# Upper conditioning groups as VectorE sums, bias with the small vectors, two context banks opened by halves

## Chip, cores and metric

The kernel runs on one core of a Trainium2 chip. Its time is the device time of one execution in microseconds; lower is better. The time before is the median of three runs.

## The reference

One layer (DEPTH = 1) of a trunk over 2048 latent positions of width 1024, with 256 context positions in front. The part that the change touches is the conditioning at the start:

```
ada   = silu(c)     @ w_ada + b_ada      # six vectors of 1024: sh1, sc1, g1, sh2, sc2, g2
ada_c = silu(c_ctx) @ w_ada + b_ada      # csh1, csc1, ... for the context
hc = rmsnorm(ctx, norm_mix) * (1 + csc1) + csh1
hf_c, hb_c = states of the scans over  hc @ w_in[:, :3*512]
h  = rmsnorm(x, norm_mix) * (1 + sc1) + sh1
x  = x + g1 * (token_mixers(h @ w_in, start states hf_c, hb_c) @ w_out)
...                                      # then the gated MLP with a 3x3 convolution, and a final RMSNorm
```

So nothing can be multiplied by w_in before shift (sh1) and scale (sc1) are there, and the context comes first: its two states start the latents' scans.

## The kernel before

**Conditioning.** The columns of w_ada for shift and scale are four groups of 512: groups 0 and 1 are the shift's lower and upper half, 2 and 3 the scale's. Each is loaded as two tiles of 1 MB (`load_ada`, L252). The two vectors silu(c) and silu(c_ctx) stand in `cs2`, index w = 1 for the context. Groups 0, 2 and 3 are products on TensorE with two rows out (`ada_products`, L263); `ada_columns` (L269) adds the bias row on VectorE, transposes the sum into columns and `put_ada` (L282) writes them into `s1` (shift) or `a1` (scale, times the norm's gain). Group 1 is summed on VectorE (`ada_sums`, L276): for each of eight k one scalar_tensor_tensor for w = 0 and one for w = 1 into `acc`, whose first partition is loaded with the bias; eight products with a matrix of ones then sum over partitions. A pair of columns k = 0 to 3 of 128 features needs groups 0 and 2, and k = 4 to 7 needs groups 1 and 3.

**Context.** Two tiles of context rows are squared on ScalarE (`x_square`), scaled on VectorE (`x_scale`, L227) and transposed into four PSUM banks (`pct`). `ctx_mod` (L293) applies shift and scale to column k (`x_mod`: `xfl`, L232, on VectorE), rounds it to fp32r on ScalarE (`ch`, L120) and takes the rest as `cl` (L121), on GpSimd for k below 4 and on VectorE above. All products are three fp32r products of such high and low parts. `split_w` does the same for 128 columns of w_in: `whi` on ScalarE, `wlo` on VectorE or GpSimd.

**Banks.** `run_banks` (L481) then goes through a list of output banks: twelve of the context, each 24 products of 256 columns (`pj<-ch,...`), among them from the seventh on the first of the latent (`pj<-xh,...`, 512 columns). Between products it calls `slot()`, which runs tasks of two queues (`hg_q`, `bg_q`) when the sum of modelled product times has come to their due time. One task, `x_start` with `x_first` (L371), squares, scales (`xg`, L227), transposes and modulates the first 1024 latent rows.

**Order.** The start stands in a block `manual_schedule`, where the written order is kept for the instructions of that block; what comes after it is placed by a scheduler, engine by engine, and may also be placed between the block's instructions. Loads of weights and rows go through SyncE's queue, the small vectors through ScalarE's. A `raw` buffer (three of them) holds context rows at first and weights of w_in after.

Of the kernel before, what the change touches and what calls it, by code (L numbers as in the profile page):

```python
# [9 lines left out]
F32 = mybir.dt.float32  # L10
# [62 lines left out]
def tile_trunk(ctx, tc, x, c, cx, c_ctx, w_ada, b_ada, norm_mix, norm_ffn, w_in, hg_norm, sgu_g, sgu_b,  # L73
# [104 lines left out]
    with es1:  # L178
# [70 lines left out]
        acc = ph.tile([P, 2, 512], F32, tag="S", name="acc")  # L249
        G.memset(acc, 0.0)  # L250

        def load_ada(g, qs=(0, 1)):  # L252

            for q in (qs,) if isinstance(qs, int) else qs:
                t = wa[g // 2][:, 4 * (g % 2) + 2 * q:4 * (g % 2) + 2 * q + 2, :]
                wts[g, q] = t.rearrange("p a (b e) -> p (a b) e", e=512)
                ld(wts[g, q], wv[:, 4 * q:4 * q + 4, g * 512:(g + 1) * 512])

        def load_bias(g, tag):
            rows[g] = pm.tile([2, 512], F32, tag=tag, name="rows", bufs=2)  # L260
            ld(rows[g], b_ada[0:1, g * 512:(g + 1) * 512].broadcast_to([2, 512]))
# [6 lines left out]

        def ada_columns(g):  # L269
            V.tensor_add(rows[g], rows[g], pa.pop(g)[:2, :])  # L270
            pv = bank("pj")
            for j in range(4):
                T.transpose(pv[:, 2 * j:2 * j + 2], rows[g][:, j * P:(j + 1) * P], ident[:2, :2])
            put_ada(g, [pv[:, w:8:2] for w in range(2)])

        def ada_sums(k0, k1):  # L276
            for k in range(k0, k1):
                for w in range(2):
                    V.scalar_tensor_tensor(out=acc[:, w, :], in0=wts[1, k // 4][:, k % 4, :], scalar=cs2[:, k, w:w + 1],
                                           in1=acc[:, w, :], op0=ALU.mult, op1=ALU.add)  # L280

        def put_ada(g, cols):  # L282
            sl = slice(4 * (g % 2), 4 * (g % 2) + 4)
            for w in range(2):
                if g < 2:
                    V.tensor_copy(s1[:, w, sl], cols[w])
                else:
                    V.scalar_tensor_tensor(out=a1[:, w, sl], in0=cols[w], scalar=1.0, in1=nmix[:, sl],
                                           op0=ALU.add, op1=ALU.mult)
# [4 lines left out]
        def ctx_mod(k, eng):  # L294
            x_mod(pct[k // 2][:, (k % 2) * 256:(k % 2) * 256 + 256], 1, k, chl[:, k, :], cll[:, k, :], CTX, eng)
# [4 lines left out]
        with tc.manual_schedule():  # L300
# [3 lines left out]
            vr = pm.tile([50, P], F32, tag="gu", name="vr", bufs=2)  # L304
            for a, n, r0 in ((norm_mix[0], 8, 0), (norm_ffn[0], 8, 8), (hg_norm[0], 4, 16), (sgu_g[0], 4, 20),
                             (sgu_b[0], 4, 24), (conv_b[0], 22, 28)):
# [5 lines left out]
            load_bias(0, "ot")  # L312
            for w in range(2):
                ld(acc[0:1, w, :], b_ada[0:1, 512:1024])
            load_bias(3, "vv")
            load_ada(3)
            load_raw((0, CTX))
# [5 lines left out]
            pv = bank("sc")  # L323
            T.transpose(pv[:, :50], vr, ident[:50, :50])
            V.tensor_copy(vec, pv[:, :50])
            ada_products(2, 1)
            ada_columns(2)
            x_scale(xc, ss, keep=lambda i: i)
            ada_sums(0, 4)
            ada_products(0, 0)  # L330
# [4 lines left out]
            load_raw((HW, CTX))  # L335
            ada_products(0, 1)
            ada_columns(0)
            ada_sums(4, 5)
            for k in range(4):
                ctx_mod(k, G)  # L340
                if k == 1:
                    ada_sums(5, 6)
            ada_products(3, 0)
# [3 lines left out]
            ada_sums(6, 8)  # L347
# [1382 lines left out]
```

## Time and profile before

| | |
|---|---|
| median of three runs | 2520.57 us (2520.07 to 2527.65) |
| the profiled execution, its own time | 2514.66 us |
| its span | 2512.8 us, mean granted TensorE clock 0.991 |
| PE busy | 2442.2 us (97%) |
| DVE busy | 1800.0 us (72%) |
| ACT, POOL busy | 957.3 us (38%), 1055.6 us (42%) |
| DMA | 400.13 MB, mean 159 GB/s |
| first context product on PE | 43.03 us from the span's start |

How to read it: the span runs from the first instruction to the last of one profiled execution. PE is TensorE (matmul), DVE VectorE, ACT ScalarE, POOL GpSimd, SP SyncE. A timeline row gives start, duration, engine, line, operation, output and inputs by the program's names, shapes and count; the bracket gives the idle time before it and what ended that. A row of windows gives for a stretch each engine's busy time with its number of instructions, then the granted TensorE clock (PEclk, 1.00 is full), the DMA engines' share and the rate. A product of fp32 shows as two MATMUL instructions, one of fp32r as one.

### The profile page before, as it was taken

The page shows a single profiled execution, that of the slowest core. Times are in us where ns is not written, and L with a number is a line of the kernel's source. Part 1 is how long each engine was busy: PE and PEld are TensorE (multiplying, and loading weights), DVE is VectorE, ACT ScalarE, POOL GpSimd, SP SyncE. Part 2 cuts the span into 40 slices and gives each one's busy share as a digit, 9 for nine tenths or more (in the row PEclk, how much of TensorE's full clock was granted, in tenths as well). Part 3 has the DMA queues.
Part 4 walks back from the last instruction along what each step waited for, and adds up shares of the span by engine and source line. Part 5 has one row for each costly group of instructions (what it writes and reads, how often), then busy time and mean ns, then how long its engine had stood idle before and what let it go on. Part 6 is the DMA issues. An engine that isn't in the chain of part 4 may idle for free.

```text
span 2512.8 us, 32811 instructions
## 1 busy us (share of the span) xinstructions
PE 2442.2 (97%) x11859; PEld 2021.4 (80%) x11859; DVE 1800.0 (72%) x2375; ACT 957.3 (38%) x1598; POOL 1055.6 (42%) x871
## 2 busy tenths in 40 slices
PE   7999999999999999999999999999999999999998
PEld 4787888788888788788778888878878887888886
DVE  5867875745665666465799778759999993676775
ACT  2553334433334343245443333324333343332352
POOL 1344232232333333100588787877878870000002
PEclk8999999999999999999999999999999999999999
DMA  8365445573353422668832222472222249844744
GB/s 293 96 194 181 131 130 193 177 248 126 101 180 104 148 88 97 237 210 256 301 106 87 90 79 89 148 261 85 82 92 87 94 134 343 275 148 134 232 159 149
DMA packets 307839, 400.13 MB, mean 159 GB/s; under 512 B 33106, under 2 KB 216138, under 8 KB 304606
## 3 DMA queue, kind: packets, MB, share of 16 engines
q1 hardware_dynamic: 304420, 397.30, 47.6%
q8 instruction: 94, 1.54, 0.2%
q10 hardware_dynamic: 3257, 0.75, 0.1%
q14 instruction: 68, 0.55, 0.1%
HBM read 288.85 MB, written 109.13 MB: 158 GB/s over the span
## 4 chain that ended last, share of the span: by engine, by line
PE 38%; DVE 7%; DMA 3%; POOL 2%; issue 2%; ACT 0%; SPq 0%; POOLq 0%; ACTq 0%; DVEq 0%
PE up L65 24%; PE dn L65 14%; DVE dn L1318 4%; DMA mr<-m 1%; DVE edges L1323 1%; DMA raw<-in_w_up_dram 1%; POOL Al L121 1%; DVE gp L1394 0%; DMA yl<-yd 0%; DMA sT<-wd 0%; DVE mhl L121 0%; DVE odd L1598 0%; POOL raw L1145 0%; POOL fl L1141 0%; ACT dn L1615 0%
## 5 line engine op out<-in xcount | busy, mean ns | idle before, releaser
L1318 DVE SCALAR_TENSOR_TENSOR dn<-gp,taps,dn 128x1024 f32<-128x1024 f32 x352 | 448.3, 1280 | 20.6 <-ACT dn L1315 17.4
L121 POOL TENSOR_TENSOR Al<-raw,Ah 128x512 fp32r<-128x512 f32 x264 | 344.9, 1315 | 97.5 <-ACT Ah L120 91.3
L65 PE MATMUL pj<-xh,whi 128*128 128x512 f32 x896 | 364.7, 407 | 0.5 <-ACT xh L120 0.5
L65 PE MATMUL pj<-xl,whi 128*128 128x512 f32 x896 | 351.2, 392 | 1.9 <-DVE xl L121 1.1
L65 PE MATMUL pj<-xh,wlo 128*128 128x512 f32 x896 | 350.9, 392 | 1.0 <-DVE wlo L121 1.0
L65 PE MATMUL dn<-th,mhl 128*128 128x512 f32 x1120 | 347.4, 391 | 2.2 <-ACT mhl L120 0.9
L65 PE MATMUL up<-xah,Ah 128*128 128x512 f32 x704 | 277.0, 394 | 1.6 <-ACT Ah L120 1.2
L65 PE MATMUL up<-xah,Al 128*128 128x512 f32 x704 | 276.3, 392 | 1.8 <-POOL Al L121 1.8
L65 PE MATMUL up<-yl,Ah 128*128 128x512 f32 x704 | 274.5, 390 | 1.9 <-DMA yl<-yd 1.9
L120 ACT CAST Ah<-raw 128x512 fp32r<-128x512 f32 x264 | 160.5, 618 | 296.1 <-PE up L65 236.3
L65 PEld LDWEIGHTS dn<-th,mhl 128*128 128x128 f32 x1120 | 210.2, 188 | 50.7 <-ACT mhl L120 1.3
L121 POOL TENSOR_TENSOR wlo<-raw,whi 128x1024 fp32r<-128x1024 f32 x56 | 141.2, 2522 | 226.8 <-ACT whi L120 210.3
L113 POOL TENSOR_SCALAR rs<-ss 128x2 f32<-128x2 f32 (+1 forms) x16 | 7.7, 481 | 526.6 <-ACT jk L1590 361.4
L65 PE MATMUL dn<-tl,mhl 128*128 128x512 f32 x560 | 219.8, 392 | 0.0
L65 PE MATMUL up<-yh,Ah 128*128 128x512 f32 x528 | 208.1, 394 | 0.0
L65 PE MATMUL up<-yh,Al 128*128 128x512 f32 x528 | 206.9, 392 | 0.0
L65 PE MATMUL up<-xal,Ah 128*128 128x512 f32 x528 | 205.5, 389 | 0.0
L65 PEld LDWEIGHTS pj<-xh,wlo 128*128 128x128 f32 x896 | 168.5, 188 | 37.6 <-DVE wlo L121 1.7
L65 PEld LDWEIGHTS pj<-xh,whi 128*128 128x128 f32 x896 | 169.4, 189 | 34.3 <-issue 3.5
L65 PEld LDWEIGHTS pj<-xl,whi 128*128 128x128 f32 x896 | 169.3, 189 | 33.2 <-DVE xl L121 2.1
L65 PE MATMUL dn<-wo,o 128*128 128x512 f32 x768 | 182.6, 394 | 0.9 <-DVE nt L672 0.9
L65 PEld LDWEIGHTS dn<-wo,o 128*128 128x128 f32 x768 | 142.0, 188 | 30.1 <-issue 1.1
(321 smaller groups left out, 4675.0 us busy)
## 6 DMA issues: line engine op xcount, KB each, us to landing
raw<-in_w_up_dram SPq DMA_DIRECT2D x88, 512.0 KB
mr<-m SPq DMA_DIRECT2D x85, 512.0 KB
raw<-in_w_in_dram SPq DMA_DIRECT2D x68, 512.0 KB
sT<-wd SPq DMA_DIRECT2D x88, 256.0 KB
raw<-in_w_ada_dram SPq DMA_DIRECT2D x32, 512.0 KB
m<-cv SPq DMA_DIRECT2D x22, 544.0 KB
raw<-in_w_down_dram SPq DMA_DIRECT2D x22, 512.0 KB
wd<-raw SPq DMA_DIRECT2D x22, 512.0 KB
```

The source lines that it names most:

```text
L65: return self.engine.matmul(out, lhsT, rhs, **kw)
L113: keep(G.tensor_scalar(out=r[:, :n], in0=ss, scalar1=scale, scalar2=bias, op0=ALU.mult, op1=ALU.add))
L120: keep(S.copy(hi, raw))
L121: (eng or G).tensor_sub(lo, raw, hi.bitcast(F32))
L1318: V.scalar_tensor_tensor(out=cr, in0=gt[:, t // 3:t // 3 + RH, t % 3:t % 3 + GW], scalar=taps[:, t * NF + f:t * NF + f + 1], in1=cr, op0=A ...
L1323: V.scalar_tensor_tensor(out=e[:, 0, :], in0=gt[:, 1, t % 3:t % 3 + GW], scalar=taps[:, t * NF + f:t * NF + f + 1], in1=e[:, 0, :], op0=AL ...
```

## The change

Groups 1 and 3 are both summed on VectorE now, separately for the context's vector (w = 1) and the latent's (w = 0), each with ones products of its own (`ada_ones`); the two accumulators stand in `acc[1]` and `acc[3]`. Groups 0 and 2 stay on TensorE, and ScalarE copies their rows. The bias of all four groups is loaded with the small vectors (`vr`, now 66 rows), transposed with them and kept in columns (`bc`), where `put_ada` adds it. The latent's sums of group 3 are written behind the block as five tasks of `hg_q` (`last_sums`).

The context's lower columns (k below 4) are modulated and rounded on ScalarE; all `cl` are on VectorE. The first two context banks (columns 0 and 512) are opened with k = 0 to 3 inside the block (`ctx_products`), and `run_banks` finishes them with k = 4 to 7. Their weights are split on VectorE, and loaded ahead of groups 1 and 3.

```diff
-        acc = ph.tile([P, 2, 512], F32, tag="S", name="acc")
-        G.memset(acc, 0.0)
+        acc = {1: ph.tile([P, 2, 512], F32, tag="S", name="acc1"),
+               3: view(ph.tile([P, NCH + 1, P], F32, tag="bst", name="acc3"), 0, [[512, 2], [1, 512]])}
+        for g in (1, 3):
+            G.memset(acc[g], 0.0)
...
+                for k in range(0, 4, 2 if (g, q) == (3, 1) else 4):
+                    e = 4 if (g, q) != (3, 1) else k + 2
+                    ld(wts[g, q][:, k:e, :], wv[:, 4 * q + k:4 * q + e, g * 512:(g + 1) * 512])
...
+        def ada_rows(g, tag):
+            rows[g] = pm.tile([2, 512], F32, tag=tag, name="rows", bufs=2)
+            S.copy(rows[g], pa.pop(g)[:2, :])
+
         def ada_columns(g):
-            V.tensor_add(rows[g], rows[g], pa.pop(g)[:2, :])
-            pv = bank("pj")
+            o = 128 + 16 * g
             for j in range(4):
-                T.transpose(pv[:, 2 * j:2 * j + 2], rows[g][:, j * P:(j + 1) * P], ident[:2, :2])
-            put_ada(g, [pv[:, w:8:2] for w in range(2)])
+                T.transpose(small[:, o + 2 * j:o + 2 * j + 2], rows[g][:, j * P:(j + 1) * P], ident[:2, :2])
+            put_ada(g, small[:, o:o + 8].rearrange("p (j w) -> p w j", w=2), 0, 2)
-        def ada_sums(k0, k1):
+        def ada_sums(g, w, k0, k1):
             for k in range(k0, k1):
-                for w in range(2):
-                    V.scalar_tensor_tensor(out=acc[:, w, :], in0=wts[1, k // 4][:, k % 4, :], scalar=cs2[:, k, w:w + 1],
-                                           in1=acc[:, w, :], op0=ALU.mult, op1=ALU.add)
+                V.scalar_tensor_tensor(out=acc[g][:, w, :], in0=wts[g, k // 4][:, k % 4, :], scalar=cs2[:, k, w:w + 1],
+                                       in1=acc[g][:, w, :], op0=ALU.mult, op1=ALU.add)
+        def ada_ones(g, w, to, o):
+            for j in range(4):
+                T.matmul(to[:, o + 2 * j:o + 2 * j + 2], acc[g][:, w, j * P:(j + 1) * P], ones[:, :2], start=True, stop=True)
+            put_ada(g, to[:, o:o + 8].rearrange("p (j u) -> p u j", u=2)[:, :1, :], w, w + 1)
+        def put_ada(g, cols, w0, w1):
             sl = slice(4 * (g % 2), 4 * (g % 2) + 4)
+            dst = (s1, a1)[g // 2][:, w0:w1, sl]
+            V.tensor_add(dst, cols, view(bc, 4 * g, [[0, w1 - w0], [1, 4]]))
+            if g > 1:
+                V.tensor_mul(dst, dst, view(vec, sl.start, [[0, w1 - w0], [1, 4]]))
...
-        def ctx_mod(k, eng):
-            x_mod(pct[k // 2][:, (k % 2) * 256:(k % 2) * 256 + 256], 1, k, chl[:, k, :], cll[:, k, :], CTX, eng)
+        def ctx_mod(k):
+            pt = pct[k // 2][:, (k % 2) * 256:(k % 2) * 256 + 256]
+            sc, sh = a1[:, 1, k:k + 1], s1[:, 1, k:k + 1]
+            fl = pm.tile([P, 512], F32, tag="sig", name="xfl", bufs=2)
+            if k < 4:
+                S.activation(fl[:, :CTX], pt, AF.Identity, bias=sh, scale=sc)
+                S.copy(chl[:, k, :], fl[:, :CTX])
+            else:
+                V.tensor_scalar(out=fl[:, :CTX], in0=pt, scalar1=sc, scalar2=sh, op0=ALU.mult, op1=ALU.add)
+                S.activation(chl[:, k, :], pt, AF.Identity, bias=sh, scale=sc)
+            V.tensor_sub(cll[:, k, :], fl[:, :CTX], chl[:, k, :].bitcast(F32))
...
-            load_bias(2, "ot")
-            for q in range(2):
-                load_ada(0, q)
-                load_ada(1, q)
...
+            load_ada(0)
+            load_raw((0, CTX))
+            load_ada(1)
+            load_raw((HW, CTX))
             load_ada(3)
-            load_raw((0, CTX))
...
             ada_products(2, 1)
+            ada_rows(2, "ot")
+            x_scale(xc, ss, keep=lambda i: i)
+            ada_products(0, 0)
             ada_columns(2)
...
+            nxt[0, CTX] = split_w((0, CTX), V)
             (16 transposes of the context)
             ada_products(0, 1)
+            ada_rows(0, "ot")
+            ada_sums(1, 1, 0, 8)
             ada_columns(0)
+            ada_ones(1, 1, small, 256)
+            for c in (0, HW):
+                opened[c, CTX] = bank("pj")
             for k in range(4):
+                ctx_mod(k)
+                ada_sums(1, 0, 2 * k, 2 * k + 2)
+                ctx_products(0, (k,))
+            nxt[HW, CTX] = split_w((HW, CTX), V)
+            ctx_products(HW, range(4))
+            ada_ones(1, 0, small, 272)
             load_raw((2 * HW, CTX))
...
+            ada_sums(3, 1, 0, 8)
+            ada_ones(3, 1, small, 288)
             for k in range(4, NK):
+                ctx_mod(k)
+        last_sums = [lambda k=k: ada_sums(3, 0, k, k + 2) for k in range(0, 8, 2)]
+        last_sums.append(lambda: ada_ones(3, 0, bank("mi"), 0))
...
+                pj = opened.pop(keys[i], None)
+                k0 = 0 if pj is None else 4
+                pj = pj or bank("pj")
...
+        for i in range(5):
+            hg_q.later(sums_now, 1.0 + 2.0 * i)
```

More of the change, by code (lines that the diff above doesn't have):

```diff
@@ L297, in tile_trunk, with ctx_products @@
+        opened = {}
+        def ctx_products(c, ks):
+            hi, lo, _ = nxt[c, CTX]
+            pj = opened[c, CTX]
+            for k in ks:
+                mm3(pj[:, :CTX], hi[:, k, :], lo[:, k, :], chl[:, k, :], cll[:, k, :], k == 0, False)
         xg = [ph.tile([P, D], F32, tag=t, name="xg", bufs=2) for t in ("vt", "vt", "sgt", "sgt")]
@@ L495, in run_banks @@
                 hiT, loT = (chl, cll) if n == CTX else (xh, xl)
-                pj = bank("pj")
+                pj = opened.pop(keys[i], None)
+                k0 = 0 if pj is None else 4
+                pj = pj or bank("pj")
                 sl = slice(n0, n0 + n)
-                for k in range(NK):
+                for k in range(k0, NK):
                     if k and n == 512:
```

56 lines of the change are left out of this document (14 added, 42 removed).

## The prediction

> **What bounds the kernel now.** I read the page first, for the limit of the whole, then the windows, for the stage that the change touches, then the timelines of PE, DVE, ACT and POOL there.
>
> ```profile
> span 2512.8 us, 32811 instructions
> PE 2442.2 (97%) x11859; PEld 2021.4 (80%) x11859; DVE 1800.0 (72%) x2375; ACT 957.3 (38%) x1598; POOL 1055.6 (42%) x871
> ```
> PE is the limit of the whole, with some 70 us idle. What delays PE early and is not made up stays in the end time.
>
> ```profile
> core 0: us, PE busy (x) PEld busy (x) DVE busy (x) ACT busy (x) POOL busy (x), PEclk, DMA share, GB/s
> 5.00:20.00 15.00, 12.39 (x27) 2.41 (x28) 2.44 (x6) 2.30 (x4) 0.92 (x2) 1.00 1.04 402
> 20.00:43.00 23.00, 17.94 (x67) 7.98 (x65) 17.44 (x24) 2.57 (x5) 6.92 (x5) 0.91 1.06 371
> 43.00:60.00 17.00, 16.34 (x84) 15.10 (x85) 9.52 (x21) 10.42 (x21) 0.19 (x1) 0.62 0.42 137
> 60.00:80.00 20.00, 16.65 (x118) 14.35 (x117) 18.62 (x28) 14.05 (x25) 11.19 (x6) 1.00 0.42 125
> 80.00:100.00 20.00, 17.43 (x104) 13.66 (x102) 17.80 (x30) 7.26 (x15) 6.42 (x6) 1.00 0.24 65
> ```
> To 43 us DMA is full; DVE has room before 20 (2.44 of 15) and is near its limit from 20 to 43. From 43 to 60 PE multiplies the context banks, at 0.62 of its clock. From 60 to 100 DVE is nearly full (18.62 and 17.80 of 20): the latent chain.
>
> ```profile
> start us, us, engine line op out<-in xcount [idle before <-releaser]
> 12.90 3.60 PE L65 MATMUL pj<-wa,cs 128*2 128x512 f32 x8
> 17.26 0.41 PE L69 MATMUL pj<-ident,rows 2*128 2x2 f32 x4 [0.77 <-DVE rows L270]
> 21.12 1.53 PE L69 MATMUL mi<-ident,raw 128*128 128x128 f32 x12
> 39.04 3.54 PE L65 MATMUL pj<-ones,acc 128*128 128x2 f32 x16 [3.56 <-POOL wlo L121]
> 43.84 0.41 PE L65 MATMUL pj<-ch,whi 128*128 128x256 f32 x1
> 44.05 0.41 PE L65 MATMUL pj<-cl,whi 128*128 128x256 f32 x1
> 55.56 0.41 PE L65 MATMUL pj<-ch,wlo 128*128 128x256 f32 x1
> 55.77 0.37 PE L65 MATMUL pj<-ch,whi 128*128 128x256 f32 x1
> 56.09 0.28 PE L65 MATMUL pj<-ch,wlo 128*128 128x256 f32 x1
> 56.21 0.28 PE L65 MATMUL pj<-ch,whi 128*128 128x256 f32 x1
> 74.29 0.48 PE L65 MATMUL pj<-xh,whi 128*128 128x512 f32 x1
> ```
> Starts of neighbours give the price of one context product: 0.21 us at 44, 0.12 at 56. The second bank's last (the 48th) starts at 55.56, the first latent product at 74.29.
>
> ```profile
> 22.09 5.39 DVE L279 SCALAR_TENSOR_TENSOR acc<-wa,cs,acc 128x512 f32<-128x512 f32 x8 [2.83 <-DMA acc<-in_b_ada_dram]
> 34.98 4.62 DVE L279 SCALAR_TENSOR_TENSOR acc<-wa,cs,acc 128x512 f32<-128x512 f32 x3
> 39.52 0.67 DVE L270 TENSOR_TENSOR rows<-rows,pj 2x512 f32<-2x512 f32 x1
> 43.13 0.23 DVE L288 SCALAR_TENSOR_TENSOR a<-pj,vec 128x4 f32<-128x4 f32 x2 [2.94 <-PE pj L69]
> 43.61 0.55 DVE L232 TENSOR_SCALAR xfl<-mi,a,s 128x256 f32<-128x256 f32 x1
> 44.62 0.43 DVE L121 TENSOR_TENSOR cl<-xfl,ch 128x256 fp32r<-128x256 f32 x1 [0.47 <-ACT ch L120]
> 44.97 0.54 DVE L232 TENSOR_SCALAR xfl<-mi,a,s 128x256 f32<-128x256 f32 x1
> 49.63 1.23 DVE L121 TENSOR_TENSOR wlo<-raw,whi 128x1024 fp32r<-128x1024 f32 x1 [0.52 <-ACT whi L120]
> 61.15 2.74 DVE L227 TENSOR_SCALAR xg<-xg,rs 128x1024 f32<-128x1024 f32 x4 [0.91 <-POOL rs L115]
> 241.79 1.53 DVE L872 SCALAR_TENSOR_TENSOR acc<-raw,cs,acc 128x512 f32<-128x512 f32 x2
> ```
> This is the chain to 43 us: sums that wait for a bias row until 22.09, then run slowly beside POOL (three in 4.62 us), then ones products and small copies, then the upper context columns (xfl) from 43.61, 1.36 us each.
>
> **The change part by part.** Of the changed kernel I use only the order in which its instructions stand on each engine. From about 100 us on the two orders are the same, so the change is worth what it moves before that: nothing behind is tied to a fixed time, and whom PE waits for there is as late as PE.
>
> *Removed:* group 3's two sets of PE products (2 x 3.6 us by the row at 12.90), three row additions of 0.67 us on DVE, the bias transfers with the 2.83 us stall, and POOL's subtractions, which slowed the sums. *Added on DVE:* 16 more sums, four cl subtractions and one wlo subtraction that POOL had. That is 16 x 0.66 + 4 x 0.34 + 1.2 = 13.2 us, less 4 x 0.45 for lower xfl that go to ACT and 2.0 for row additions: 9.4 us net, on the engine that the upper columns queue on. What stands against this is DVE's idle time before 43.
>
> Sums that alternate between two accumulators start 0.66 us apart (5.39 - 0.74, over 7); two on one accumulator take 1.53 for the pair, 0.79 apart.
>
> *Walk to the lower columns.* PE's second set ends at 16.5. Group 0's first half now follows at once (3.4, the row's 3.60 less the tail of its last product): 19.9, then four transposes: 20.3. Its weights have landed: 4 MB at 402 GB/s is 10.4 us from about 5. DVE, which waited, makes a1 to 20.8 and the first wlo (1.2) to 22.0. The context's eight upper-shift sums share one accumulator: 7 x 0.79 + 0.74 = 6.3, to 28.3. Ones products: 16 instructions took 3.54 us, at half clock; eight are 1.8, or 0.9 at full clock, which PE still has here: 29.2, s1 29.4. ACT makes the lower columns' ch beside this.
>
> *Walk to the upper columns.* DVE's queue now has four groups of one cl and three sums. The third sum is one of the latent's scale: all eight of these, written to run behind, stand in the built order ahead of the upper columns. 4 x (0.34 + 3 x 0.66) = 9.3: 38.7; wlo 1.2: 39.9; two sums: 41.3. Next is s1 from the second ones products, which PE has behind the half bank opened on column 512: 12 products after that wlo. At half clock 12 x 0.21 = 2.5 and 1.8: 44.3, s1 44.5, and DVE idles 3 us with ten sums queued behind. Those ten: five alternate, five follow on one accumulator, 7.3: 51.8. Ones products 1.8, two small operations: 54.0. So the first upper xfl starts at 54.0 against 43.61. Each column again costs 1.36, since in the built order ACT's ch still waits for xfl, and PE's six products for it (6 x 0.21 = 1.28) fit beside it: the last cl ends at 59.4, the 48th product near 60.4 against 55.56: 4.9 later. The 24 products done early save this much and no more.
>
> ```profile
> 35.48:38.90 3.42, 0.00 (x1) 0.00 (x0) 3.42 (x3) 0.00 (x0) 2.91 (x2) 1.00 1.02 411
> 49.14:52.55 3.41, 2.95 (x12) 2.63 (x12) 1.23 (x1) 2.96 (x6) 0.00 (x0) 0.50 0.08 25
> 55.96:59.37 3.41, 3.41 (x31) 3.41 (x30) 2.49 (x5) 3.38 (x6) 0.00 (x0) 1.00 0.61 192
> 441.67:445.08 3.41, 0.88 (x5) 0.88 (x6) 2.68 (x4) 2.05 (x5) 0.00 (x0) 1.00 0.62 197
> 445.08:448.49 3.41, 3.41 (x16) 3.22 (x15) 3.17 (x6) 1.00 (x2) 2.78 (x1) 0.50 0.43 161
> ```
> The clock: half after a stretch in which PE was busy 0.00 of 3.42 us, but also after one with 0.88 of 3.41. Between 29 and 40 the changed PE has three products of 0.21 every 2.3 us, about as little as that 0.88; so I take half clock there, and full again at some 59 to 60.
>
> The Trainium skill ("TensorE: Matmul & The Clock Gate", Part 1: The HAM clock gate) lets the clock fall only after an idle window of about 3.4 us. By that rule it would hold until 42 here and the second ones products would end some 2 us earlier; the row at 441.67 speaks against it.
>
> *The latent chain.*
>
> ```profile
> 58.47 1.06 ACT L221 ACTIVATE xjk<-xg 128x1024 bf16<-128x1024 f32 x1
> 59.53 0.35 ACT L554 COPY vv<-pj 128x256 f32<-128x256 f32 x1
> 59.78 1.05 ACT L120 CAST whi<-raw 128x1024 fp32r<-128x1024 f32 x1
> 60.06 1.06 POOL L115 TENSOR_TENSOR rs<-rs,mhalf 128x4 f32<-128x4 f32 x1
> ```
> Before, the last square (58.47) stands ahead of the third bank's vv, and the scaling of the latent rows (xg) starts at 61.15. In the changed order the last two squares stand behind that vv. The third bank starts after its weights are split (1.05 on ACT, which waits for the first bank's buffer): 60.4 + 1.4 + 24 x 0.12 = 64.7; vv, square, split, square (0.4 + 1.2 + 1.0 + 1.2) 68.5; POOL's two operations (1.06 and a shorter one) 1.4: scaling at 69.9, 9 us later. The first latent product, which waited for both before, then comes 5 later if PE's context banks set it and 9 later if the scaling does. The second latent chunk hangs on the same DVE queue, which is full, so lateness of scaling reaches it undiminished.
>
> *At nothing:* ACT's seventh small load, 0.3 us at 3 us (PE waits for weights until 7); POOL's second memset; w_ada's last MB in two pieces; the context's first weights ahead of group 1. The second weight load now stands on SP ahead of group 3 and waits for PE's transposes (21.12): group 3 lands near 31, and DVE needs its last part near 45. Without that cover DVE would wait as long as it lacks.
>
> Sum: +4.9 at two banks, 5 to 9 at the first latent product, 9 where DVE sets the pace; I take **+9.5**, near the scaling's lateness, since DVE is the full engine from 60 to 100, with ends of +5 and +14 (POOL's and DVE's collisions, which made three sums cost 4.62 for 2.0, can hit the squeezed chain again). The profiled execution took 2514.66 us (span 2512.8); the median of the runs is 2520.57. The difference adds to either; on the median: **2530**.
>
> **The rivals.** *A, the clock holds* (the skill's rule, above): second ones products and half bank at full clock save 1.1 + 0.9; +7.5, 2528. For: PE is never idle for a whole window between 29 and 40. Against: the row at 441.67. Chance 0.15.
>
> *B, PE's slack absorbs it, and it is not slower.* PE is idle 3.35 + 2.57 = 5.9 us from 60 to 100; if PE's work and not DVE sets the latent banks, the 4.9 at two banks is swallowed: -1, 2519.6. It decides by the scaling: at 64.5 or earlier (61.15 + 3.35). For: 24 context products are done by 43. Against: DVE 18.62 of 20, and my 69.9. Chance 0.13.
>
> *C, the squeezed chain collides.* POOL's and DVE's latent splits meet as DVE's sums met POOL's split at 34.98, 2.6 us each time; two or three times more than before: +14.7 to +17.3, 2535 to 2538. For: the splits crowd behind a later scaling. Against: before has such meetings too, and its sums lose theirs here. Chance 0.12.
>
> **How the numbers follow.** Forecast 0.60. A difference of 0.3% (7.6 us) is about what a measurement of this kernel can tell from no change. Slower: 0.45 of the forecast's 0.60 (its part above +7.6), half of A (0.07), C: 0.64. Within: the other 0.15, A's 0.08, most of B: 0.33. Faster: 0.03, if B also gains what POOL no longer slows. Range 2521 to 2537: from just above B's end well into C; what it leaves out is most of B and part of C.
>
> **What would show it.** Right: first upper xfl near 54, preceded by a chain of sums without an ACT or DMA wait; half clock between 32 and 59; scaling near 70; then a constant lag. Wrong: upper xfl before 50; scaling before 64.5; full clock through 29 to 42; a DMA as releaser of a sum of group 3.

## The result, and the profile after

The changed kernel takes 2535.56 us (median of four runs, 2534.25 to 2539.13) against 2520.32 us of the kernel before on the same chip: the ratio is 1.0057, with a 95% interval of 1.0041 to 1.0073, which is 10.3 to 18.4 us. It is slower, as forecast; the forecast was +9.5. The profiled execution took 2539.13 us, the highest of its four, and that of before 2514.66, below all four of its own; the two ends are therefore not compared, but marks in the first 130 us.

The page of the changed kernel, its span and its engines:

```profile
span 2537.3 us, 32818 instructions
PE 2443.8 (96%) x11855; PEld 2021.8 (80%) x11855; DVE 1809.6 (71%) x2392; ACT 960.2 (38%) x1604; POOL 1048.4 (41%) x867
```

PE is busy about as long as before (2442.2 us there): group 3's products are gone, but more of its work runs at half clock, as the next rows show. DVE has 9.6 us more, POOL 7.2 less: the sums and subtractions that moved.

Four of the windows that were shown of before, now of the changed kernel (length, then busy time of each engine, then the granted clock, the DMA share and the rate):

```profile
core 0: us, PE busy (x) PEld busy (x) DVE busy (x) ACT busy (x) POOL busy (x), PEclk, DMA share, GB/s
20.00:43.00 23.00, 13.50 (x62) 8.89 (x61) 19.65 (x32) 6.26 (x11) 0.00 (x0) 0.73 1.02 371
43.00:60.00 17.00, 7.78 (x35) 7.39 (x35) 11.41 (x22) 1.69 (x3) 0.00 (x0) 0.50 0.43 145
60.00:80.00 20.00, 17.01 (x119) 16.04 (x119) 13.88 (x28) 13.12 (x26) 1.86 (x3) 0.88 0.34 98
80.00:100.00 20.00, 16.50 (x105) 13.27 (x104) 16.00 (x20) 12.27 (x25) 10.56 (x7) 1.00 0.21 61
```

From 43 to 60, where PE was busy for 16.34 us before, it is busy for 7.78, at half clock: it waits for the upper context columns.

DVE's timeline up to those columns, and three marks behind them (start, duration, engine, line, operation, count; in brackets the idle time before and what ended it):

```profile
21.46 1.22 DVE L121 TENSOR_TENSOR wlo<-raw,whi 128x1024 fp32r<-128x1024 f32 x1 [0.93 <-ACT whi L120]
22.85 6.26 DVE L283 SCALAR_TENSOR_TENSOR acc<-wa,cs,acc 128x512 f32<-128x512 f32 x8 [0.17 <-DMA wa<-in_w_ada_dram]
30.39 0.16 DVE L294 TENSOR_TENSOR s<-sc,bc 128x4 f32<-128x4 f32 x1 [1.21 <-PE sc L65]
30.80 2.07 DVE L283 SCALAR_TENSOR_TENSOR acc<-wa,cs,acc 128x512 f32<-128x512 f32 x3
...
39.76 1.22 DVE L121 TENSOR_TENSOR wlo<-raw,whi 128x1024 fp32r<-128x1024 f32 x1
40.90 1.53 DVE L283 SCALAR_TENSOR_TENSOR acc<-wa,cs,acc 128x512 f32<-128x512 f32 x2
45.07 0.16 DVE L294 TENSOR_TENSOR s<-sc,bc 128x4 f32<-128x4 f32 x1 [2.64 <-PE sc L65]
45.15 7.33 DVE L283 SCALAR_TENSOR_TENSOR acc<-wa,cs,acc 128x512 f32<-128x512 f32 x10
54.50 0.16 DVE L294 TENSOR_TENSOR a<-sc,bc 128x4 f32<-128x4 f32 x1 [2.02 <-PE sc L65]
54.90 0.54 DVE L310 TENSOR_SCALAR xfl<-mi,a,s 128x256 f32<-128x256 f32 x1
56.41 0.54 DVE L310 TENSOR_SCALAR xfl<-mi,a,s 128x256 f32<-128x256 f32 x1
...
73.44 2.74 DVE L227 TENSOR_SCALAR xg<-xg,rs 128x1024 f32<-128x1024 f32 x4 [1.19 <-POOL rs L115]
...
95.37 2.74 DVE L227 TENSOR_SCALAR xk<-xk,rs 128x1024 f32<-128x1024 f32 x4 [1.18 <-POOL rs L115]
...
140.69 1.22 DVE L121 TENSOR_TENSOR wlo<-raw,whi 128x1024 fp32r<-128x1024 f32 x1
```

The sums come in the forecast groups: eight, four times three, two, ten. The first upper xfl starts at 54.90 (43.61 before), the scaling of the latent rows (xg) at 73.44 (61.15), that of the second chunk of latent rows (xk) at 95.37. The last row is a split of w_in's weights. The same instruction stands in every kernel of this study, and DVE's next 500 instructions follow it in the same order. In before, the marks are

```profile
83.88 2.74 DVE L227 TENSOR_SCALAR xk<-xk,rs 128x1024 f32<-128x1024 f32 x4
...
129.11 1.22 DVE L121 TENSOR_TENSOR wlo<-raw,whi 128x1024 fp32r<-128x1024 f32 x1
```

so the changed kernel is 11.49 us late at the second chunk and 11.58 at that split. This last difference is called the **lag** below. In all kernels it keeps its value to 0.1 us between 129 and 156 us of before. Farther on, single executions drift apart: the row that stands at 999.79 in before (on<-mi,rs) is 13.29 us late in the changed kernel, and the ends are 24.5 us apart; a kernel with a lag of -4.84 ("the same, squares early" below) ends 3.3 us late against the same execution of before. So the lag is what a change does up to that mark. Whether it does more behind it, one execution of each can't tell.

Where the 11.58 arise is seen by cutting DVE's time at the first upper xfl. One row from 20 us to it, and one from it to the second chunk; first before, then changed:

```profile
20.00:43.61 23.61, 18.55 (x69) 8.57 (x68) 17.80 (x29) 2.57 (x5) 6.92 (x5) 0.90 1.05 372
...
43.61:83.88 40.27, 34.91 (x208) 30.35 (x207) 30.97 (x48) 25.73 (x48) 13.95 (x9) 0.85 0.42 127
```

```profile
20.00:54.90 34.90, 17.37 (x79) 12.62 (x77) 27.20 (x46) 6.26 (x11) 0.00 (x0) 0.65 0.88 315
...
54.90:95.37 40.47, 34.06 (x214) 30.31 (x214) 29.27 (x48) 25.09 (x48) 12.42 (x9) 0.88 0.27 78
```

Up to the columns DVE works 27.20 us instead of 17.80, which is 9.40 more, and is idle for 7.70 instead of 5.81, 1.89 more: together the 11.29 by which the columns are late. The stretch behind them is as long as before (40.47 against 40.27). Nothing of the lateness is taken back there.

### The profile page after: what moved, and what is told of

Its sections match the earlier page's. It is cut to its first block, busy times and chain, and to the rows that moved or that the text cites. A ratio compares the mean times of both kernels' runs of the same rounds, so it can differ in the third digit from the quotient of the medians.

```text
span 2537.3 us, 32818 instructions
## 1 busy us (share of the span) xinstructions
PE 2443.8 (96%) x11855; PEld 2021.8 (80%) x11855; DVE 1809.6 (71%) x2392; ACT 960.2 (38%) x1604; POOL 1048.4 (41%) x867
## 4 chain that ended last, share of the span: by engine, by line
PE 42%; DVE 6%; DMA 2%; issue 1%; POOL 1%; ACT 0%; SPq 0%; POOLq 0%; ACTq 0%
PE up L65 26%; PE dn L65 16%; DVE dn L1349 3%; DVE edges L1354 1%; DMA yl<-yd 1%; DVE gp L1425 0%; DVE odd L1629 0%; DMA sT<-wd 0%; DMA xn<-cv 0%; DMA mr<-m 0%; POOL Al L121 0%; POOL cv L1436 0%; ACT dn L1646 0%; DVE cv L1433 0%; DMA raw<-in_w_up_dram 0%
## 5 line engine op out<-in xcount | busy, mean ns | idle before, releaser
L1349 DVE SCALAR_TENSOR_TENSOR dn<-gp,taps,dn 128x1024 f32<-128x1024 f32 x352 | 448.3, 1280 | 20.6 <-ACT dn L1346 17.3
L65 PE MATMUL dn<-th,mhl 128*128 128x512 f32 x1120 | 354.2, 398 | 2.5 <-ACT mhl L120 2.5
L120 ACT CAST Ah<-raw 128x512 fp32r<-128x512 f32 x264 | 160.5, 618 | 296.3 <-PE up L65 241.2
```

What stands on the lines that cost most here:

```text
L65: return self.engine.matmul(out, lhsT, rhs, **kw)
L120: keep(S.copy(hi, raw))
L1349: V.scalar_tensor_tensor(out=cr, in0=gt[:, t // 3:t // 3 + RH, t % 3:t % 3 + GW], scalar=taps[:, t * NF + f:t * NF + f + 1], in1=cr, op0=A ...
```

## The experiments

Each ratio is to runs of the kernel before on the same chip. The table has one profiled execution of each for the marks (us from the span's start).

| kernel | first upper xfl | xg scaling | second chunk | lag | ratio, 95% interval |
|---|---|---|---|---|---|
| before | 43.61 | 61.15 | 83.88 | 0 | 1 |
| changed | 54.90 | 73.44 | 95.37 | +11.58 | 1.0057, 1.0041 to 1.0073 |
| latent's scale sums behind | 51.83 | 69.58 | 95.34 | +13.74 | 1.0054, 1.0042 to 1.0066 |
| PE kept busy | 53.73 | 71.98 | 93.89 | +10.32 | 1.0051, 1.0037 to 1.0065 |
| latent squares early | 57.41 | 47.50 | 94.64 | +10.25 | 1.0039, 1.0026 to 1.0052 |
| banks not opened by halves | 53.66 | 69.70 | 91.85 | +11.41 | 1.0050, 1.0036 to 1.0064 |
| eight more sums | 61.98 | 80.35 | 102.24 | +18.62 | 1.0083, 1.0071 to 1.0095 |
| group 3 back on TensorE | 38.83 | 65.02 | 85.34 | +1.33 | 1.0003, 0.9993 to 1.0014 |
| the same, squares early | 37.10 | 50.14 | 78.01 | -4.84 | 0.9978, 0.9968 to 0.9987 |
| the same, banks closed | 37.49 | 50.36 | 79.02 | -4.50 | 0.9973, 0.9963 to 0.9983 |
| before, squares early | 44.16 | 53.08 | 79.70 | +1.77 | 0.9998, 0.9989 to 1.0008 |
| before, bias moved | 42.04 | 58.99 | 82.15 | -2.00 | 0.9998, 0.9989 to 1.0007 |
| before, both | 42.18 | 51.09 | 77.60 | -0.01 | 1.0006, 0.9994 to 1.0018 |

The lag and the ratio go together: the ratio less 1, times 2520, is within 3 us of the lag in every row. The lag tells kernels apart that the times do not, but it is one execution of each.

**The latent's scale sums behind.** The eight sums of group 3 for w = 0 are held behind the upper columns:

```diff
+                if (g, w) == (3, 0):
+                    pin(i)
```

> The changed kernel with one thing moved: the eight sums of the latent's scale (group 3, w = 0) are held behind the upper context columns in DVE's order, where the change wrote them, instead of standing ahead. Theory (DVE's queue sets the upper columns): each of the four groups before them is one sum shorter and the ten sums before the last ones products become fewer, about 8 x 0.66 = 5 us of sums leave the chain; with the wait for the second ones products (2.6 us) growing as DVE arrives earlier, the first upper xfl starts near 50 instead of 54.9 and the time falls by 3 to 5 us against the changed kernel. The sums then fall into the latent chain, where DVE is full, so some of it comes back: if all 5 us come back there, the total stays. Rival (PE's half clock sets it): the wait grows by as much as the sums shrink, xfl stays at 54 to 55, no change.

The columns come 3.07 us earlier, and the ratio stays. The windows show the exchange:

```profile
20.00:51.83 31.83, 18.54 (x81) 13.52 (x80) 22.35 (x37) 6.27 (x11) 0.00 (x0) 0.64 0.98 346
...
51.83:95.34 43.51, 34.76 (x210) 30.87 (x211) 33.88 (x56) 25.32 (x47) 11.44 (x9) 0.87 0.25 73
```

DVE works 4.85 us less ahead of the columns (22.35 against 27.20) and 4.61 more behind them (33.88 against 29.27); the second chunk comes at 95.34 against 95.37. That the scheduler had put these sums ahead was therefore not the loss: DVE's queue sets both stretches, and what leaves the one lengthens the other. Behind the second chunk 2.2 us more are lost, though the last of the eight sums starts at 74.13, ahead of it; where they are lost was not followed.

**PE kept busy.** Products that nobody reads fill PE between the early context products:

```diff
+            def filler(n):
+                for _ in range(n):
+                    nc.tensor.matmul(fill[:2, :], cs2[:, 0, :], wts[2, 0][:, 0, :], start=True, stop=True)
...
+                filler(2)
                 ctx_products(0, (k,))
...
             ada_ones(1, 0, small, 272)
+            filler(8)
```

> The changed kernel with unused fp32 products of 512 columns put on PE between the early context products (two ahead of each of the four, eight behind the second ones products), so that PE is busy and its clock can stay full from 30 to 52 us. Theory of the clock: the second ones products, the half bank and the third bank run at full clock, s1 near 43 instead of 45.1, the first upper xfl near 52 to 53, the third bank's vv 2 us earlier still: 3 to 5 us less than the changed kernel. Theory of DVE's queue: the sums set it, the clock is worth only the idle 2.6 us before s1: 0 to 3 us less. If the granted clock stays at half in spite of the filling, the filler itself costs up to 3 us.

The clock is at full again in the second half of this stretch (windows of this kernel):

```profile
30.00:43.00 13.00, 13.00 (x40) 4.75 (x41) 11.71 (x20) 4.03 (x8) 0.00 (x0) 0.81 1.01 368
43.00:54.00 11.00, 9.66 (x40) 3.83 (x38) 8.12 (x15) 0.00 (x0) 0.00 (x0) 1.00 0.70 241
```

The columns come 1.17 us earlier and the lag falls by 1.26; the ratio doesn't tell it from the changed kernel. What is gained lies in DVE's second and third wait for ones products, 2.64 and 2.02 us, which are 1.42 and 1.21 now, as the theory of DVE's queue has it; the first wait is longer, 2.02 for 1.21. The filling itself takes PE's time, so a full clock that cost nothing could be worth more.

**Latent squares early.** The four squares of the latent rows stand on ScalarE ahead of the upper columns, where it is idle for 20 us:

```diff
+            ss_g = x_sums()
+            for q in range(2):
+                for i in range(2):
+                    jk = pm.tile([P, D], BF16, tag="acc", name="xjk")
+                    S.activation(jk, xg[2 * q + i], AF.Square, accum_out=ss_g[:, 2 * q + i:2 * q + i + 1])
             ada_sums(3, 1, 0, 8)
```

> The changed kernel with the four squares of the latent rows put on ScalarE ahead of the upper columns, where ScalarE is idle for 20 us, instead of behind the third bank's vv. Theory (the last squares behind vv set the scaling and with it the latent chain): the scaling falls from 73.4 to some 66 to 68 us, since POOL's two operations no longer wait for squares; the first latent product comes 4 to 7 us earlier and the time falls by 4 to 7 us. Rival (DVE's and PE's context banks set the latent chain anyway): the scaling comes earlier but the first latent product stays within 2 us, and so does the time.

The scaling comes 26 us earlier, not 6: the scheduler then puts it among the ten sums, where it costs the columns 2.51 us. The lag falls by 1.33 only, and the first latent product on PE starts at 83.28 instead of 81.96, since PE has the third to sixth context banks first. The scaling at 73.44 was therefore not what held up that product. But the run does two things at once, and behind the columns it does gain:

```profile
57.41:94.64 37.23, 31.03 (x190) 28.61 (x191) 28.85 (x44) 21.24 (x39) 10.97 (x7) 0.83 0.29 85
```

The stretch to the second chunk is 3.24 us shorter (37.23 for 40.47), nearly all of it idle time of DVE (8.38 for 11.20); the 2.51 us ahead of the columns take most of that back. The ratio is lower than the changed kernel's by 0.0018, within the two intervals.

**Banks not opened by halves.**

```diff
-            for c in (0, HW):
-                opened[c, CTX] = bank("pj")
...
-                ctx_products(0, (k,))
...
-            ctx_products(HW, range(4))
```

> The changed kernel without the two context banks opened by halves: all 48 products of the first two banks come after the upper columns begin, everything else as in the change. The prediction gave the early products a worth of some 5 us (10.4 us later columns, but a 48th product only 4.9 later). By that theory the second ones products come 2.5 us earlier (nothing of the half bank ahead of them), the upper xfl 1 to 2 us earlier, the 48th product 3 to 5 us later, and the time 2 to 5 us above the changed kernel. Rival: in this order ScalarE has the squares ahead of the third bank's vv, so the scaling comes earlier than 73.4, and the time is 0 to 4 us below the changed kernel; then the half banks were worth less than the order that they brought.

The lag is 11.41 against 11.58, and the ratio is not told apart. But the edit did not do what it was meant to do: the early products are still early. In the changed kernel the first and the last of them, and the last product of the first two banks, are

```profile
30.28 0.38 PE L65 MATMUL pj<-ch,whi 128*128 128x256 f32 x1
...
43.12 0.41 PE L65 MATMUL pj<-ch,wlo 128*128 128x256 f32 x1
...
61.63 0.28 PE L65 MATMUL pj<-ch,wlo 128*128 128x256 f32 x1
```

With the banks closed the first and the last before the upper columns are

```profile
29.81 0.56 PE L65 MATMUL pj<-ch,whi 128*128 128x256 f32 x1
...
43.31 0.41 PE L65 MATMUL pj<-ch,wlo 128*128 128x256 f32 x1
```

and both kernels have 24 context products there. `run_banks` stands behind the block, and the scheduler places its products of k below 4 between the block's instructions. So this run tells what it costs to write the products elsewhere (nothing that can be told), and not what 24 early products are worth. The expectation that all 48 would follow the upper columns did not come true.

**Eight more sums**, into an accumulator that is not read, ahead of the last ones products:

```diff
+            for k in range(8):
+                V.scalar_tensor_tensor(out=dose, in0=wts[3, k // 4][:, k % 4, :], scalar=cs2[:, k, 0:1], in1=dose,
+                                       op0=ALU.mult, op1=ALU.add)
             ada_sums(3, 1, 0, 8)
```

> The changed kernel with eight more sums on VectorE ahead of the last ones products, of the same form and from the same weights, into an accumulator that nobody reads. Measures by itself what a sum in that place costs. Theory (VectorE's queue sets the upper columns, and these set the end): first upper xfl 5.3 to 6.3 us later (8 x 0.66 to 0.79), and the time 5 to 7 us above the changed kernel. Rival (slack of TensorE or of the latent chain takes it up): the columns come as late, the time rises by under 3 us.

```profile
20.00:61.98 41.98, 18.77 (x82) 13.36 (x80) 33.63 (x56) 6.35 (x11) 0.00 (x0) 0.62 0.75 264
```

DVE works 6.43 us more (33.63 against 27.20); the columns are 7.08 later and the lag 7.04 larger. Not all of it is sums: two casts of 0.42 us (msk), which stand behind the first upper xfl in the changed kernel, come ahead of it here, and DVE starts on the sums 0.49 us later. That leaves some 5.9 us for the eight, 0.74 each. The ratio rises by 0.0026, 6.6 us. What makes the columns late here costs the end its full length, as the theory has it.

**Group 3 back on TensorE.** Its products follow those of group 0, its weights are loaded ahead of the second bank's; group 1 alone is summed, its context share ahead, its latent share behind the columns:

```diff
-            ada_ones(1, 1, small, 256)
+            ada_products(3, 0)
+            ada_products(3, 1)
...
-                ada_sums(1, 0, 2 * k, 2 * k + 2)
...
+            ada_rows(3, "vv")
+            ada_ones(1, 1, small, 256)
+            ada_columns(3)
...
-            ada_sums(3, 1, 0, 8)
-            ada_ones(3, 1, small, 288)
...
-        last_sums = [lambda k=k: ada_sums(3, 0, k, k + 2) for k in range(0, 8, 2)]
+        last_sums = [lambda k=k: ada_sums(1, 0, k, k + 2) for k in range(0, 8, 2)]
```

> The changed kernel with group 3 (upper columns of the factor) back on TensorE, both halves for both vectors, its weights loaded ahead of the second context bank's; only group 1 is summed on VectorE, the context's share ahead, the latent's behind the upper columns; both context banks are opened by halves after the lower columns, the bias stays with the small vectors. 16 sums and 9 to 10 us leave DVE's chain and 7 us of PE products come back where PE is idle. Theory (DVE's queue is the loss): the first upper xfl falls from 54.9 to some 35 to 44 us, which is no later than before (43.6), and the time is 10 to 25 us below the changed kernel, 0 to 10 us below the kernel before. Rival (the loss is in the latent chain, whatever the upper columns do): within 5 us of the changed kernel.

The columns come 16.07 us earlier, with 24 sums fewer ahead of them (0.67 for each), and the lag falls by 10.25, with 16 sums fewer in all (0.64 for each). The other eight stand behind the columns now and take their part back: the columns are 4.78 us earlier than before, and the time is that of before. Behind the columns this kernel is slower than before:

```profile
38.83:85.34 46.51, 37.64 (x236) 33.08 (x236) 34.50 (x55) 24.96 (x47) 11.42 (x9) 0.89 0.48 146
```

46.51 us against 40.27, of which DVE works 3.53 more and is idle 2.71 more. Some 2.1 of the 3.53 are the scaling of xg, which takes 4.83 us here and 2.74 in before and in the changed kernel: POOL splits weights beside it (wlo, from 66.48 to 69.29). The theory of this run held for its main part (the 16 sums are the loss); of the 0 to 10 us that it gave over the kernel before, nothing is seen.

**The same, squares early**: two squares ahead of the upper columns, one behind each of the first two.

```diff
+            ss_g = x_sums()
+            x_square(xg[:2], ss_g, 0, keep=lambda i: i)
             for k in range(4, NK):
                 ctx_mod(k)
+                if k < 6:
+                    x_square(xg[k - 2:k - 1], ss_g, k - 2, keep=lambda i: i)
```

> The kernel with group 3 back on TensorE (the one of the run before), and now also the four squares of the latent rows early on ScalarE: two ahead of the upper columns, one behind each of the first two of them. In that run the upper columns were 4.8 us earlier than in the kernel before, and yet the time was the same, with the scaling of the latent rows 3.9 us later (65.02 against 61.15), because the squares stand on ScalarE behind the third bank's vv and between the evictions of the cumulative sums. Theory (the squares' place sets the scaling, and the scaling gives back what the columns gain): scaling at 49 to 52, first latent xfl at 58 to 62 instead of 71.4, time 4 to 10 us below that run and below the kernel before. Rival (TensorE's context banks and VectorE's queue fill the time anyway): within 3 us of both.

```profile
37.10:78.01 40.91, 33.60 (x221) 29.67 (x221) 34.10 (x56) 23.80 (x45) 11.39 (x9) 0.92 0.58 184
```

The stretch falls from 46.51 to 40.91 us with nearly the same work of DVE (34.10 against 34.50): idle time of 12.01 has become 6.81, and the scaling of xg takes 2.74 us again. This kernel beats both, 0.9978 of before. On the changed kernel the four squares shortened this stretch by 3.24 us, but there the scheduler put the scaling ahead of the upper columns, which paid 2.51 for it; here it stands behind them, at 50.14, and they are not later (37.10 against 38.83).

**The same, banks closed**: the kernel of the last run without the halves.

```diff
-            for c in (0, HW):
-                opened[c, CTX] = bank("pj")
...
-            ctx_products(0, range(4))
-            ctx_products(HW, range(4))
```

> The fastest kernel so far (group 3 on TensorE, latent squares early) without the two context banks opened by halves. Theory (the half banks save TensorE time when the columns come early, since there TensorE and not VectorE is the next limit): upper columns unchanged at about 37 us, the 48th product 2 to 3 us later, time 2 to 5 us above that kernel. Rival (as in the changed kernel, where closing them cost nothing): within 2 us.

It is at 0.9973, median 2513.83 against 2519.15 us, the fastest of the study, and not told apart from the last by its interval. As on the changed kernel, the edit did not make the products late: they start at 35.76, against 36.59 with the halves, and ten of them stand ahead of the first upper xfl instead of four. So the halves need not be written; what the early products are worth stays untested.

**Before, squares early; before, bias moved; before, both.** The first is the edit above on the kernel before, the second

```diff
-            V.tensor_add(rows[g], rows[g], pa.pop(g)[:2, :])
+            rows[g] = pm.tile([2, 512], F32, tag=tag, name="rows", bufs=2)
+            S.copy(rows[g], pa.pop(g)[:2, :])
...
+            V.tensor_add(dst, cols, view(bc, 4 * g, [[0, 2], [1, 4]]))
```

with the bias among the small vectors; the third is both.

> The kernel before with one thing moved: the four squares of the latent rows, two ahead of the upper columns, one behind each of the first two. ScalarE is idle there for 8.8 us. If the place of the squares is worth something by itself, without any part of the change, scaling falls from 61.15 to some 52 to 55 us and the time by 2 to 6 us. If the latent chain waits for TensorE or for VectorE's wlo splits, the scaling moves and the time stays within 2 us.

> The kernel before with only the bias moved: it comes with the small vectors, the row copies go to ScalarE, all products and sums, the order of loads and the closed banks stay. The prediction's terms for this part were 2.83 us of VectorE's wait for a bias row and three row additions of 0.67 us, 4.8 us ahead of the upper columns at most. Theory (VectorE's queue to the upper columns sets the end, one for one as the eight further sums showed): upper xfl some 2 to 4 us earlier than 43.61 and the time 2 to 4 us below the kernel before. Rival (group 3's products on TensorE, which wait for their weights until 39, set the upper columns there): upper xfl and time within 1.5 us.

> The run before this with the latent squares early as well. Alone they gave nothing on the kernel before (scaling 8 us earlier, time the same), on the kernel with group 3 on TensorE they gave 6 us. If what makes them worth something is that the columns are early, this gains no more than the bias alone gives, plus 0 to 2 us; if it is the latent's sums that stand behind, it gains nothing over the bias alone.

None is told apart from before by its time. With the squares early the second chunk is 4.18 us earlier, and the lag 1.77 later: the next stretch takes it back.

```profile
83.88:129.11 45.23, 43.22 (x260) 36.34 (x259) 35.08 (x68) 20.45 (x40) 13.08 (x10) 1.00 0.32 102
```

```profile
79.70:130.88 51.18, 45.73 (x265) 38.68 (x266) 37.24 (x67) 20.63 (x39) 15.36 (x11) 0.97 0.32 100
```

Before is the first, with PE busy for 43.22 of 45.23 us; with early squares PE is idle for 5.45 of 51.18 us there. One part of the 5.95 us by which this stretch is longer can be seen. The scaling of the second chunk now meets a split on POOL:

```profile
79.64 2.33 POOL L121 TENSOR_TENSOR wlo<-raw,whi 128x1024 fp32r<-128x1024 f32 x1
79.70 4.81 DVE L227 TENSOR_SCALAR xk<-xk,rs 128x1024 f32<-128x1024 f32 x4 [0.90 <-POOL rs L115]
```

It takes 4.81 us for 2.74, which is 2.07 more. The same meeting stands at 91.85 in the changed kernel with closed banks and at 77.60 in "before, both", with 4.81 us each. The rest was not taken apart. The bias alone brings the columns 1.57 us earlier, less than its theory's 2 to 4, and the lag to -2.00; the interval of its times (-2.8 to +1.8 us) holds both that and nothing. Both together show no gain in the time, and a lag that is 2 us above that of the bias alone. That is in line with the second reading set down for this run (the latent's sums behind are what makes squares worth something), but the meeting just shown costs as much, so the run does not decide it.

## Why the prediction was right, and where it was off

Direction, mechanism and place were right: slower, because the upper columns queue on DVE behind more sums. The size was short by some 2 us against the trace (9.5 for 11.58) and by 5.7 against the medians (interval 0.8 to 8.9). That it came this near is luck in part: the lateness of 9 that it was taken from is not what sets the pace, and it was itself short (12.29). Step by step:

**Walk to the columns.** First upper xfl at 54.0, measured 54.90. The ledger of DVE's work (13.2 added, less 3.8 removed: 9.4) has the sum that the windows show, 27.20 - 17.80 = 9.40, but its terms differ and make up for each other. The rows of the sums from 20 us to the first upper xfl, before and changed (busy time, then the mean of one in ns):

```profile
L279 DVE SCALAR_TENSOR_TENSOR acc<-wa,cs,acc 128x512 f32<-128x512 f32 x16 | 14.4, 960 | 2.8 <-DMA acc<-in_b_ada_dram 2.8
L283 DVE SCALAR_TENSOR_TENSOR acc<-wa,cs,acc 128x512 f32<-128x512 f32 x32 | 22.9, 747 | 0.6 <-DMA wa<-in_w_ada_dram 0.2
```

Sixteen more sums are 8.5 us more and not 10.6, because those of before were slowed by POOL, which the ledger named but did not count. Two splits of weights stand ahead of the columns (2.4 us), where the ledger had one: in before DVE's first stands behind them, at 49.63. The groups were 6.3, 9.3 and 7.3 us long in the forecast; measured are 6.26, 9.29 (30.47 to 39.76) and 7.33. The wait for the second ones products was put at 3, and is 2.64. What is 0.9 late came early: wlo waits for ScalarE's whi (0.93), which waits for its weights until 20.38.

**The clock.** Half was forecast from some 32 to 59 or 60; the profile has it from 30.57 to 61.29, and once more after that:

```profile
23.75:27.16 3.41, 2.20 (x9) 0.49 (x7) 3.27 (x5) 0.57 (x1) 0.00 (x0) 1.00 1.06 354
27.16:30.57 3.41, 1.24 (x9) 1.15 (x9) 2.13 (x6) 1.32 (x3) 0.00 (x0) 1.00 1.03 382
30.57:33.98 3.41, 1.82 (x7) 1.43 (x6) 3.41 (x7) 2.10 (x6) 0.00 (x0) 0.50 1.09 371
...
57.88:61.29 3.41, 3.41 (x15) 3.16 (x16) 2.23 (x6) 1.13 (x2) 0.00 (x0) 0.50 0.00 0
61.29:64.70 3.41, 1.88 (x13) 1.47 (x13) 1.39 (x2) 3.11 (x7) 0.00 (x0) 1.00 0.00 0
...
64.70:68.11 3.41, 3.41 (x18) 3.41 (x18) 2.75 (x6) 2.06 (x4) 0.00 (x0) 0.50 0.53 154
```

In these rows the clock stays full after a window of 3.41 us with 2.20 busy, is half after 1.24, full after 3.41 and half after 1.88. That is no rule on the busy share: later in the same execution it stays full after a window with 1.62 busy.

```profile
743.98:747.39 3.41, 1.62 (x9) 0.91 (x7) 2.51 (x3) 1.63 (x2) 2.73 (x3) 1.00 0.10 32
747.39:750.81 3.42, 3.05 (x24) 2.94 (x25) 3.42 (x5) 0.59 (x1) 0.00 (x0) 1.00 0.54 190
```

The Trainium skill ("TensorE: Matmul & The Clock Gate", Part 1: The HAM clock gate) has full rate after a busy window and half after an idle one. The rows at 57.88 and 61.29 agree with the first, though in before a window with 3.41 busy (from 42.31) is followed by one more at half clock. But half came here without an idle window too: PE was busy for more than half of the window of 61.29. So rival A failed on its condition. The filled kernel, with the cost of its filling in it, gains 1.26 us, where A was given 2.0.

**A column** was put at 1.36 us and takes 1.51: ScalarE makes ch from PSUM and takes 0.56 us for it, as in the first of ScalarE's rows below; the cast of the kernel before took 0.40 (ch, L120). DVE waits for it, and four columns end 0.6 us later than forecast for that.

**The 24 early products** were to save "this much and no more": 5.5 of the 10.4 us by which the columns are late, so that the 48th product, and with it one end of the range, came at +4.9. At that place the term is about right: the last of the 48 starts at 61.63 against 55.56, 6.07 later, while the columns are 11.29 later. What failed is its use as an end of the range: of these 5.2 us nothing is left at the second chunk (11.49). No run shows what the end would be without the early products, since the two kernels with closed banks have them as well.

**The latent chain.** Scaling was forecast at 69.9, and is at 73.44, in the forecast order. ScalarE's rows:

```profile
55.48 0.56 ACT L311 ACTIVATE ch<-mi,s,a 128x256 fp32r<-128x256 f32 x1 [20.28 <-DVE xfl L310]
...
68.38 0.37 ACT L583 COPY vv<-pj 128x256 f32<-128x256 f32 x1 [1.62 <-PE pj L65]
68.64 1.06 ACT L221 ACTIVATE xjk<-xg 128x1024 bf16<-128x1024 f32 x1
```

vv was put at 64.7 and comes at 68.38. By the 48th product 1.2 us of this are there (61.63 for 60.4). The third bank takes most of the rest: its products run 0.21 us apart instead of 0.12 in the window of 64.70, at half clock, where the forecast had full, and it waits 0.76 us for its wlo. The first latent product comes 7.67 us later (81.96 against 74.29), within the 5 to 9 that were forecast. But the step that failed is the conclusion "9 where DVE sets the pace; I take +9.5, near the scaling's lateness", with the lateness of scaling reaching the second chunk undiminished. With the squares early, scaling is 25.94 us earlier and the stretch behind the columns only 3.24 shorter, so it is not the scaling that sets the pace there. The columns' lateness does, nearly one for one, where the order behind them is left as it is: 7.08 and 7.04 with eight more sums, 1.17 and 1.26 with PE busy. With that step right the forecast's own walk (54.0 against 43.61) gives +10.4.

**The account of DVE.** The lag is the columns' lateness, plus the sums left to stand behind them: 11.29 for 11.58 in the changed kernel; 10.12 for 10.32 with PE busy; 18.37 for 18.62 with eight more; -4.78 + 8 x 0.66 to 0.79, 0.5 to 1.5, for 1.33 with group 3 on TensorE; -1.57 for -2.00 with the bias alone. With the sums behind it gives 8.22 + 8 x 0.66 = 13.5 for 13.74, but not by its own reasoning: the second chunk is no later there, and 2.2 us arise behind it. It is 1.2 to 1.4 short in the three kernels where the scaling of the second chunk takes 2.07 us longer beside POOL (the changed kernel with closed banks, 10.05 for 11.41, and the two kernels of before with squares early). And it fails where the squares are early on the changed kernel (13.80 for 10.25) and where they are early with group 3 on TensorE (-1.2 to -0.2 for -4.84, and much the same with closed banks): there DVE's idle time behind the columns falls too, and that the account leaves out.

**Rivals B and C.** B (PE's slack takes it up from a scaling of 64.5 on) has its condition met with the squares early, at 47.50, and the time is still 1.0039: PE's slack does not absorb the loss. C (two or three more meetings of POOL and DVE, +14.7 to +17.3) is not seen in the changed kernel's trace: the stretch in which they were to fall is as long as before (40.47 against 40.27). Meetings of a scaling and a split did turn up in four other kernels of the study, at some 2.1 us each, where C gave 2.6. The median, 15.2 higher, lies in C's range; what the lag does not show of it, 3.6 us, is less than the interval is wide (10.3 to 18.4), and stays open.

## What to carry over

Before work is moved to an engine that is idle on the average, cut that engine's time at the point for which the next engine waits, and keep an account on either side of it: the work that is moved ahead of that point counts in full, and what is put behind it counts again if the engine is full there too. An instruction that both kernels have, found behind the last difference of order, tells in one trace what the change is worth up to there, here to within 3 us of the timed difference. What is done early on another engine may only move a wait: the four squares shortened one stretch of the changed kernel by 3.24 us and lengthened the one ahead by 2.51, and gave 0.25% once group 3 had left VectorE. And before a run is read as a test, look in its trace whether the edit moved what it was to move: closing the banks left all 24 early products early.

## What was not expected of the hardware

The sums cost 741 to 753 ns each in the changed kernel, where POOL does nothing beside them, and up to 2823 ns before, beside POOL's split (the rows of the two lines by operation):

```profile
L283 DVE SCALAR_TENSOR_TENSOR acc<-wa,cs,acc x32: 741/746/753, 22.8 to 51.7; 128x512 f32<-128x512 f32 x32
```

```profile
L279 DVE SCALAR_TENSOR_TENSOR acc<-wa,cs,acc x16: 740/747/2823, 22.1 to 38.9; 128x512 f32<-128x512 f32 x16
```

One window with PE busy for 1.88 of 3.41 us was followed by half clock in the whole of the next; one with 1.62, later in the same execution, was not. An ACTIVATE with scale and shift from PSUM to fp32r took 0.56 us for 128x256, where a cast of the same size from SBUF took 0.40.
